# A sparse 3x3 convolution on one core: every image stored in two halves of 32 rows, and the last pair's load issued whole with the others

## The chip, the cores and the metric

The kernel runs on one core of a Trainium2 chip. Its time is the device time of one execution in microseconds. Three executions of the kernel before took 127.68, 127.80 and 127.81 us, median 127.8 us.

## The reference

Sixteen images of 64 channels and 64 x 64 pixels are convolved with 128 filters of 3 x 3, padded by one. Nine weights in ten are zero, but the kernel multiplies by all of them. All inputs and outputs are 32-bit floats in HBM.

```python
batch, c_in, h, w, c_out, k = 16, 64, 64, 64, 128, 3
x_pad = np.pad(x, ((0, 0), (0, 0), (1, 1), (1, 1)))
for b, co, ci, kh, kw in all_indices:
    output[b, co] += weight[co, ci, kh, kw] * x_pad[b, ci, kh:kh+h, kw:kw+w]
```

## The kernel before, in words

**Pairs and blocks.** The images are worked off in eight pairs, p = 0 to 7. The 64 channels of the pair's two images fill the 128 partitions, and each image uses half of TensorE's rows. Each image is cut into four blocks of 16 rows. A block called "T" (`twos`, L151) computes even and odd output rows apart: GpSimd (POOL) adds neighbouring rows of x (L154, tile `s`), TensorE multiplies (L135), ScalarE (ACT) copies the shared product to SBUF (L161, tile `pc`), and VectorE (DVE) adds it to the rest and writes the output tile `o` (L168). The first block of pair 0 goes a direct way (`direct`, L144).

**Loads.** Pair 0's upper half is loaded as floats by SyncE's queue (SP, L62) and cast by engines. Everything else of x is loaded by GpSimd's queue with a cast to 16 bits on the way: pair 0's lower half (L63), pairs 1 to 6 whole (L67), all issued at the start; then pair 7, whose three DMAs (L177 to L181) stand in the program at the head of pair 2, and so in GpSimd's stream behind the row additions of pair 1. They load the upper half of the rows for all 128 partitions, and the lower half once for partitions 0 to 7 and once for partitions 8 to 127. Every pair has its own x tile, so no load waits for a buffer.

**Stores.** An image's output is a tile of 128 partitions x 64 x 64 floats, 2 MB, 16 KB in each partition. There are seven such buffers (pool `o`, L47); the first holds the head of x at the start, and image j uses buffer (j + 1) modulo 7, so image j can be written only when the stores of image j - 7 have landed. Images of pairs 0 to 6 are stored whole behind the pair's last block (L193 to L195). Only the two images of pair 7 go in halves of 32 rows, each behind its second and fourth block (L189 to L192). All stores go through SyncE's queue, which also waits there for VectorE.

**Order.** The scheduling is manual: every engine works in the order of the program, and only the waits on semaphores tie them. The transfers of both queues run on the same 16 DMA engines. On the SP queue a store uses one of eight completion semaphores in turn.

Of the kernel before, what the change touches and what calls it, by code (L numbers as in the profile page):

```python
# [27 lines left out]
def kernel(  # L28
# [6 lines left out]
    nc = tc.nc  # L35

    B, C_IN, H, W = x.shape
    C_OUT, _, KH, KW = weight.shape
    assert (B, C_IN, H, W) == (16, 64, 64, 64) and (C_OUT, KH, KW) == (128, 3, 3)
    NP = B // 2  # L40
# [14 lines left out]
    def pair(p):  # L55
        return x[2 * p : 2 * p + 2].rearrange("n i h w -> (n i) h w")

    xs = [x_pool.tile([128, H, W], BF16, name=f"x{p}") for p in range(NP)]
# [4 lines left out]
    nc.gpsimd.dma_start(out=xs[0][:, HEAD:H, :], in_=pair(0)[:, HEAD:H, :])  # L63
    ident = const_pool.tile([128, 128], BF16, name="ident")
    make_identity(nc, ident)
    for p in range(1, NP - 1):
        nc.gpsimd.dma_start(out=xs[p], in_=pair(p))  # L67


# [74 lines left out]
    def direct(p, o, r0, rows):  # L144
        ps = product(
            [(xs[p], G1, r0, 1), (xs[p], G0, r0 - 1, 1), (xs[p], G2, r0 + 1, 1)], rows
        )
        nc.scalar.copy(out=o[0][:, r0 : r0 + rows, :], in_=ps[0])  # L148
        nc.vector.tensor_copy(out=o[1][:, r0 : r0 + rows, :], in_=ps[1])  # L149

    def twos(p, o, r0):  # L151
        t0 = r0 // 2
        s = s_pool.tile([128, 8, W], BF16, name="s")
        nc.gpsimd.tensor_tensor(  # L154
            out=s, in0=xs[p][:, r0 : r0 + 16 : 2, :], in1=xs[p][:, r0 + 1 : r0 + 16 : 2, :], op=ADD
        )
        shared = product([(s, G1, 0, 1)], 8)
        pc = []
        for n in range(2):
            c = p_pool.tile([128, 8, W], FP32, name="pc")  # L160
            nc.scalar.copy(out=c, in_=shared[n])  # L161
            pc.append(c)
        even = [(xs[p], G21, r0 + 1, 2), (xs[p], G0, r0 - 1, 2)]
        odd = [(xs[p], G01, r0, 2), (xs[p], G2, r0 + 2, 2)]
        for first, terms in ((r0, even), (r0 + 1, odd)):
            ps = product(terms, 8)
            for n in range(2):
                nc.vector.tensor_tensor(  # L168
                    out=o[n][:, first : r0 + 16 : 2, :], in0=ps[n], in1=pc[n], op=ADD
                )  # L170

    for p in range(NP):
        o = [o_pool.tile([C_OUT, H, W], FP32, name="o") for _ in range(2)]
        last = p == NP - 1
        if p == 2:
            x_last, half = pair(NP - 1), H // 2
            nc.gpsimd.dma_start(out=xs[NP - 1][:, 0:half, :], in_=x_last[:, 0:half, :])  # L177
            for a, b in ((0, 8), (8, 128)):
                nc.gpsimd.dma_start(  # L179
                    out=xs[NP - 1][a:b, half:H, :], in_=x_last[a:b, half:H, :]  # L180
                )  # L181
        for blk in range(4):
            r0 = 16 * blk
            if BLOCKS[p][blk] == "T":
                twos(p, o, r0)
            else:
                for r, rows in ((r0, 8), (r0 + 8, 8)):
                    direct(p, o, r, rows)
            if last and blk % 2 == 1:  # L189
                for n in range(2):  # L190
                    rows = slice(r0 - 16, r0 + 16)
                    nc.sync.dma_start(out=out[2 * p + n][:, rows, :], in_=o[n][:, rows, :])  # L192
        if not last:  # L193
            for n in range(2):
                nc.sync.dma_start(out=out[2 * p + n], in_=o[n])  # L195


# [28 lines left out]
```

## Time and profile before

| | |
|---|---|
| median of three executions | 127.8 us |
| the profiled execution: time | 127.8 us |
| the profiled execution: span, first to last instruction | 126.0 us |
| granted TensorE clock, mean | 0.958 |
| TensorE matmul busy | 110.5 us (88%) |
| VectorE, ScalarE, GpSimd busy | 82.3, 38.9, 41.8 us |
| HBM read, written | 17.07 MB, 33.55 MB |
| a whole-image store, from issue to landing (median of 14) | 17.6 us |
| a half-image store (median of 4) | 10.1 us |

Times in the views are microseconds from the span's start. In the page's strip of 40 slices one slice is 3.15 us; its line DMA gives the mean busy share of the 16 DMA engines in tenths, and GB/s what they moved, where a load that is cast counts with its 16-bit size only, half of what it reads. PE is TensorE, SPq and POOLq are the instruction queues of SyncE and GpSimd that issue DMAs. A DMA is cut into packets of one partition's row each; beside the views the trace keeps a record of every packet (queue, start, duration, size) and of every completion, and numbers said to be of the packet records are read there.

### The profile page before, as it was taken

The page shows a single profiled execution, that of the slowest core. Times are in us where ns is not written, and L with a number is a line of the kernel's source. Part 1 is how long each engine was busy: PE and PEld are TensorE (multiplying, and loading weights), DVE is VectorE, ACT ScalarE, POOL GpSimd, SP SyncE. Part 2 cuts the span into 40 slices and gives each one's busy share as a digit, 9 for nine tenths or more (in the row PEclk, how much of TensorE's full clock was granted, in tenths as well). Part 3 has the DMA queues.
Part 4 walks back from the last instruction along what each step waited for, and adds up shares of the span by engine and source line. Part 5 has one row for each costly group of instructions (what it writes and reads, how often), then busy time and mean ns, then how long its engine had stood idle before and what let it go on. Part 6 is the DMA issues. An engine that isn't in the chain of part 4 may idle for free.

```text
span 126.0 us, 2489 instructions
## 1 busy us (share of the span) xinstructions
PE 110.5 (88%) x1002; PEld 56.0 (44%) x1002; DVE 82.3 (65%) x135; ACT 38.9 (31%) x71; POOL 41.8 (33%) x47
## 2 busy tenths in 40 slices
PE   6679999999999999999999999999999999990000
PEld 6434445544555455545554555445544554440000
DVE  0352277777777777877787778777877787773000
ACT  4541532333333333333333333333333333330000
POOL 6846333383333333333333333333333330000000
PEclk9999999999999999999999999999999999998555
DMA  4999999999999999999999999999999999999980
GB/s 140 343 229 211 216 213 216 221 164 296 325 335 302 325 296 371 344 376 351 367 412 426 421 432 432 437 429 416 421 437 437 411 400 437 437 390 413 432 343 21
DMA packets 4220, 42.93 MB, mean 341 GB/s; under 512 B 496, under 2 KB 496, under 8 KB 1008
## 3 DMA queue, kind: packets, MB, share of 16 engines
q1 hardware_dynamic: 2880, 34.90, 65.9%
q0 software_dynamic: 1328, 7.87, 30.9%
q8 instruction: 8, 0.13, 0.4%
q14 instruction: 4, 0.03, 0.1%
HBM read 17.07 MB, written 33.55 MB: 402 GB/s over the span
## 4 chain that ended last, share of the span: by engine, by line
PE 83%; DMA 4%; DVE 1%; issue 1%; DVEq 0%; SPq 0%
PE ps L135 83%; DMA o<-in_x_dram 4%; DVE o L168 1%; DVEq L221 0%; DVE x L87 0%; SPq L60 0%; DVEq L168 0%
## 5 line engine op out<-in xcount | busy, mean ns | idle before, releaser
L135 PE MATMUL ps<-x,wT 64*128 64x504 bf16 (+3 forms) x780 | 91.5, 382 | 1.6 <-DVE x L87 1.6
L168 DVE TENSOR_TENSOR o<-ps,pc 128x512 f32<-128x512 f32 x124 | 77.8, 685 | 22.1 <-PE ps L135 19.8
L135 PEld LDWEIGHTS <-wT 64*128 64x128 bf16 x966 | 52.5, 96 | 55.2 <-issue 5.0
L154 POOL TENSOR_TENSOR s<-x 128x512 bf16<-128x512 bf16 x31 | 35.6, 1151 | 59.5 <-PE ps L135 46.7
L161 ACT COPY pc<-ps 128x512 f32<-128x512 f32 x62 | 33.3, 589 | 64.0 <-issue 61.8
L135 PE MATMUL ps<-s,wT 64*128 64x512 bf16 (+1 forms) x186 | 25.5, 377 | 0.0
L149 DVE COPY o<-ps 128x512 f32<-128x512 f32 x2 | 1.4, 692 | 4.9 <-PE ps L135 4.9
L74 PE MATMUL ps<-idle_rhs 128*128 128x128 bf16 x27 | 3.1, 310 | 1.0 <-DVE idle_rhs L71 1.0
L74 PEld LDWEIGHTS <-idle_rhs 128*128 128x128 bf16 x27 | 2.8, 144 | 1.0 <-DVE idle_rhs L71 1.0
L67 POOL DMA_DIRECT2D x<-in_x_dram x6 | 3.2, 560 | 0.0
L91 DVE CAST w_bf<-w_sb 128x192 bf16<-128x192 f32 (+1 forms) x4 | 1.1, 361 | 2.7 <-DMA w_sb<-in_weight_dram 2.7
L148 ACT COPY o<-ps 128x512 f32<-128x512 f32 x2 | 1.2, 585 | 5.3 <-PE ps L135 5.3
L87 ACT CAST x<-o 128x576 bf16<-128x576 f32 (+1 forms) x2 | 1.5, 802 | 0.6 <-DMA o<-in_x_dram 0.6
L87 DVE CAST x<-o 128x576 bf16<-128x576 f32 x1 | 0.5, 459 | 1.7 <-DMA o<-in_x_dram 1.7
L91 ACT ACT_TABLE_LOAD x1 | 1.3, 1283 | 0.7 <-PEq L210 0.7
L97 PE MATMUL ps<-ident,w_bf 128*128 128x128 bf16 x9 | 1.2, 308 | 0.1
L91 ACT CAST w_bf<-w_sb 128x64 bf16<-128x64 f32 (+1 forms) x2 | 0.7, 418 | 1.6 <-DMA w_sb<-in_weight_dram 1.6
L179 POOL DMA_DIRECT2D x<-in_x_dram x2 | 1.1, 530 | 0.0
L97 PEld LDWEIGHTS <-w_bf 128*128 128x128 bf16 x9 | 0.8, 127 | 0.6 <-DVE w_bf L91 0.6
L101 DVE TENSOR_TENSOR wT<-ps,wT 128x384 bf16<-128x384 f32 x2 | 1.0, 546 | 0.0
L63 POOL DMA_DIRECT2D x<-in_x_dram x1 | 0.7, 710 | 0.8 <-POOLq L210 0.8
L71 DVE MEMSET idle_rhs<- 128x64 uint32 x1 | 0.1, 112 | 0.8 <-PEq L210 0.8
(10 smaller groups left out, 3.0 us busy)
## 6 DMA issues: line engine op xcount, KB each, us to landing
out_dram<-o SPq DMA_DIRECT2D x14, 2048.0 KB, 17.6
x<-in_x_dram POOLq DMA_DIRECT2D x6, 1024.0 KB, 23.9
out_dram<-o SPq DMA_DIRECT2D x4, 1024.0 KB, 10.1
o<-in_x_dram SPq DMA_DIRECT2D x1, 1024.0 KB, 5.3
x<-in_x_dram POOLq DMA_DIRECT2D x2, 512.0 KB, 20.2
x<-in_x_dram POOLq DMA_DIRECT2D x1, 480.0 KB, 40.3
w_sb<-in_weight_dram SPq DMA_DIRECT2D x1, 288.0 KB, 2.9
x<-in_x_dram POOLq DMA_DIRECT2D x1, 32.0 KB, 33.4
```

What stands on the lines that cost most here:

```text
L67: nc.gpsimd.dma_start(out=xs[p], in_=pair(p))
L74: nc.tensor.matmul(idle_ps, idle_rhs, idle_rhs, start=True, stop=True)
L87: copy(out=xs[0][:, a:b, :], in_=x_head[:, a:b, :])
L91: copy(out=w_bf4[:, g, a:b, :], in_=w_v[:, k : k + b - a, :])
L97: nc.tensor.matmul(wps[:, j, :], src, ident, start=True, stop=True)
L135: nc.tensor.matmul(ps[n][:, lo:hi, c_lo:c_hi], tap(g, kw, n), src[q, a:b:step, c_lo + kw - 1 : c_hi + kw - 1], start=(i == 0), stop=(i == ...
L148: nc.scalar.copy(out=o[0][:, r0 : r0 + rows, :], in_=ps[0])
L149: nc.vector.tensor_copy(out=o[1][:, r0 : r0 + rows, :], in_=ps[1])
L154: nc.gpsimd.tensor_tensor(out=s, in0=xs[p][:, r0 : r0 + 16 : 2, :], in1=xs[p][:, r0 + 1 : r0 + 16 : 2, :], op=ADD)
L161: nc.scalar.copy(out=c, in_=shared[n])
L168: nc.vector.tensor_tensor(out=o[n][:, first : r0 + 16 : 2, :], in0=ps[n], in1=pc[n], op=ADD)
L179: nc.gpsimd.dma_start(out=xs[NP - 1][a:b, half:H, :], in_=x_last[a:b, half:H, :])
```

## The change

All seven later pairs are now loaded at the start by the loop at L66, each with one DMA; the three DMAs at the head of pair 2 are gone. Every image is stored in two halves, where only pair 7's were: behind a pair's second block two DMAs send rows 0 to 31 of both images, and behind its fourth block two more send rows 32 to 63. There are 32 stores of 1 MB in place of 14 of 2 MB and 4 of 1 MB.

```diff
-    for p in range(1, NP - 1):
+    for p in range(1, NP):
         nc.gpsimd.dma_start(out=xs[p], in_=pair(p))
...
         o = [o_pool.tile([C_OUT, H, W], FP32, name="o") for _ in range(2)]
-        last = p == NP - 1
-        if p == 2:
-            x_last, half = pair(NP - 1), H // 2
-            nc.gpsimd.dma_start(out=xs[NP - 1][:, 0:half, :], in_=x_last[:, 0:half, :])
-            for a, b in ((0, 8), (8, 128)):
-                nc.gpsimd.dma_start(
-                    out=xs[NP - 1][a:b, half:H, :], in_=x_last[a:b, half:H, :]
-                )
...
-            if last and blk % 2 == 1:
+            if blk % 2 == 1:
                 for n in range(2):
                     rows = slice(r0 - 16, r0 + 16)
                     nc.sync.dma_start(out=out[2 * p + n][:, rows, :], in_=o[n][:, rows, :])
-        if not last:
-            for n in range(2):
-                nc.sync.dma_start(out=out[2 * p + n], in_=o[n])
```

## The prediction

> **What bounds the kernel now.** I read the page's strip first. PE is full from 7 to 113 us, but the DMA line is full from 3 to 122 us, and after the last matmul the engines move bytes for some ten microseconds more.
>
> ```profile
> PE   6679999999999999999999999999999999990000
> DMA  4999999999999999999999999999999999999980
> GB/s 140 343 229 211 216 213 216 221 164 296 325 335 302 325 296 371 344 376 351 367 412 426 421 432 432 437 429 416 421 437 437 411 400 437 437 390 413 432 343 21
> q1 hardware_dynamic: 2880, 34.90, 65.9%
> q0 software_dynamic: 1328, 7.87, 30.9%
> ```
>
> The two queues' packets take 96.8% of the 16 engines' time in the span; 216 GB/s of cast loads are 432 GB/s read. So the loads and stores, one after the other, make the time, if nothing starves them. I looked for that in SyncE's waits and then in the windows.
>
> ```profile
> SPq L195 <- DVE o L168: 93.7, 14, 22.7
> SPq L192 <- DVE o L168: 10.5, 4, 5.3
> SPq L221 <- DMA out_dram<-o: 8.8, 4, 2.4
> ```
>
> The store queue waits for VectorE, never for a buffer, and VectorE waits for no store. After the last issue the program only waits for stores (L221).
>
> ```profile
> 24.00:26.00 2.00, 2.00 (x22) 1.05 (x20) 1.40 (x3) 1.07 (x2) 1.61 (x2) 1.00 1.01 209
> 26.00:28.00 2.00, 2.00 (x22) 0.98 (x20) 2.00 (x4) 0.55 (x2) 1.55 (x4) 1.00 1.08 143
> 28.00:30.00 2.00, 2.00 (x22) 0.96 (x18) 1.27 (x4) 0.52 (x2) 0.69 (x1) 1.00 0.95 250
> 68.00:100.00 32.00, 32.00 (x302) 16.02 (x300) 25.02 (x41) 10.74 (x20) 11.53 (x10) 1.00 1.00 427
> 100.00:102.00 2.00, 2.00 (x24) 1.05 (x20) 1.77 (x3) 0.88 (x2) 0.78 (x1) 1.00 0.93 393
> 114.00:121.00 7.00, 0.00 (x0) 0.00 (x0) 0.58 (x1) 0.00 (x0) 0.00 (x0) 0.60 1.01 421
> ```
>
> The last two columns are the DMA share and GB/s. Whole-image stores run at 427 GB/s (68 to 100), half-image stores at 421 (114 to 121). There are two weak places: a dip to 143 GB/s at 26 to 28 with the engines marked busy, and a share of 0.93 at 100 to 102, just before pair 6's stores are issued (101.2). By the packet records this is one engine idle for 2.5 us and a few others for 0.3 us.
>
> ```profile
> 24.39 1.15 POOL L154 TENSOR_TENSOR s<-x 128x512 bf16<-128x512 bf16 x1 [2.02 <-PE ps L135]
> 24.42 0.88 SPq L195 DMA_DIRECT2D out_dram<-o  x2
> 25.48 0.57 POOL L177 DMA_DIRECT2D x<-in_x_dram  x1
> 26.04 1.05 POOL L179 DMA_DIRECT2D x<-in_x_dram  x2
> ```
>
> The timeline at the dip: SyncE has just issued the first stores, GpSimd issues pair 7's loads. In the packet records the 69 load packets that start between 25.3 and 29.5 take 843 ns in the mean instead of 625, up to 1515, until the first store packet starts at 28.84. That is 69 x 218 / 16 = 0.94 us lost on every engine.
>
> **The change part by part.** The sum is made on the profiled execution (127.8 us, span 126.0, so 1.8 us lie outside); it is also the median.
>
> *Stores in halves.* A store packet of 16 KB takes 614.8 ns in the mean (66 to 106 us), one of 8 KB 310.2 (116 us to the end). Each engine carries 8 rows of each of the 14 images, 112 packets, which become 224: 112 x (2 x 310.2 - 614.8) = 0.63 us; 14 more completion packets of 9 ns make 0.13. Engines that only store confirm it: one image every 4.862 us, one half every 2.453, so 14 x 0.044 = 0.61. From the windows, 29.4 MB at 421 instead of 427 GB/s is 69.8 - 68.8 = 1.0 us. I take 0.6, bounds 0 to 1.0. It lies on the path, because no engine has idle time for it. A rule of the Trainium skill speaks against halves: "DMA: Bandwidth & Descriptors", Anatomy of one DMA, gives a transfer of GpSimd's path a fixed 2.0 us besides its bytes. If each of 14 added stores paid that, the time would be 28 us longer; the half-stores at 421 GB/s above show it overlapped while more is queued.
>
> *Earlier stores.* Pair 0's first halves can go at 18.5 us (VectorE's last addition of the second block) in place of 24.4. More is queued, but a full pipe moves no more for it. The idle 0.3 us at 102 goes, on engines that do not end last: worth nothing. At the end pair 7's second halves are issued at 114.0 and 114.6 as now, and their turn comes about 2 x 2.45 before the last landing at 124.9, so at 120: 5 us of cover, nothing gained.
>
> *The order of loads.* Pair 7's load was queued behind pairs 3 to 6 already; on its queue it stays there. GpSimd issues it at 5.72 for some 0.56 us, inside 2.39 us of idle before its additions at 8.11: nothing. If issuing blocked on an eighth outstanding load it would delay TensorE from 13.75 on. The 1.6 us gone from GpSimd's stream at 25.5 end in waits for free s buffers: nothing either.
>
> *How loads and stores share.* While both run, packets alternate: at 30 to 54 us some 27 of stores to 26 of loads in 2 us. With 8 KB against 16 KB read, stores get a third of the time instead of half until the loads end. Loads come earlier (each x tile lands two pairs ahead already), stores later. By the packet records a pair's load alone takes 4.88 us, and pair 3's ends at 23.3. If the first store packet comes at 22 (some 3.5 us behind its issue; it was 4.4), 1.3 + 4 x 4.88 = 20.8 us of loads are left, so both run until 22 + 1.5 x 20.8 = 53, and 10.4 / 2.45 = 4.2 half-stores are done by then. The third lands at 44, the seventh at 60, the sixteenth at 82, one each 2.45 us. Image 9 needs image 2's buffer (the seventh) at 63.7 (VectorE begins pair 1 at 25.5 and a pair every 12.75): 3.4 us of slack, the tightest case. If that cover went, VectorE and then TensorE would stop, and 5 us at the end hide it. A store also needs its completion semaphore, used eight stores earlier: the twelfth may wait 1.5 us in SyncE with seven queued behind it on the engines, which costs nothing.
>
> *The load itself.* Three DMAs become one. A 16 KB read takes 624 ns beside stores and an 8 KB read 322, so 8 x (2 x 322 - 624) = 0.16 us less per engine. The rows of 0 to 7 that some engines carry on top go: 0 or 0.32 us, by engine. Sum -0.2, bounds 0 to -0.5. The engine spared eight rows (8 x 0.31 = 2.5 us, just its idle time at 100) gets them back and stands among the others. "DMA: Bandwidth & Descriptors", How many engines (k), says that 120 partitions of such a load can go to engines 0 to 14 alone, which would name it the sixteenth; no view here numbers engines.
>
> *The dip.* Who makes it, the trace does not say. For the first stores: it ends on each engine as its first store packet starts. Against GpSimd's issuing: the six issues of L67 end at 5.72 and the load packets of 5.3 to 7.5 take 332 ns against 324, nearly nothing. So I let it move with the first stores to about 19 us: cost 0, bounds -0.9 to +0.3 (stores and loads start up differently).
>
> Sum: 0.6 - 0.2 + 0 = +0.4, so 128.2 us; the bounds of the first terms give 127.9 to 128.6.
>
> **The rivals.**
> 1. *The dip belongs to the load that is moved.* GpSimd starts issuing at 25.48 and the first long packets start at 25.41 to 26.1. Then 0.9 us go: 128.2 - 0.9 = 127.3, faster. Against it stand the rows at 5.3 to 7.5.
> 2. *The spared engine becomes the last one.* The sixteen completions of the last store lie between 122.2 and 124.9, the second latest at 124.1: single engines are late, among them by instruction fetches of 16 KB (eight in the span, about 0.9 us each). If the engine that gets eight rows back is one of these, it ends behind them: price 0 to 2.5, taken as 0.8, so 129.0. It decides once that engine's other work is over 2 us above the others'; in the trace, less its spare, it stands in the middle.
> 3. *Nothing to be seen.* Half rows cost nothing when stores always queue deep, and the rows saved balance the rest: 127.8.
>
> **How the numbers follow.** A measurement of this kernel tells about 0.2% (0.26 us) from no change. The forecast gets 0.55, rival 1 0.25, rival 2 0.12, rival 3 0.08. Faster: rival 1 nearly whole and a little of the forecast, 0.27. Within 0.2%: rival 3, about a fifth of the forecast, a trace of rival 1, 0.20. Slower: the rest, 0.53. The range reaches to rival 1 and to most of rival 2: 127.2 to 128.9; the forecast's own is 127.9 to 128.6.
>
> **What would show it.** In the changed profile: the strip's DMA line full as now; a dip near 19 to 22 us and none at 26 (rival 1: none at all); 421 GB/s in place of 427 in the pure store stretch, which should begin near 53 instead of 65; no share of 0.93 at 100; PE ending at 112 to 113; no wait of VectorE for a store; SyncE waiting for stores once or twice near 50. A PE line with holes, a load issue of over 1 us on GpSimd, or an engine whose completions trail by over 3 us would make the prediction wrong.

## The result and the profile after

The changed kernel takes 128.43 us (median of 4, 128.38 to 128.51) against 127.81 us before on the same chip: +0.62 us, ratio 1.0045 with the 95% interval 1.0024 to 1.0066. It is slower, as forecast (+0.4), by a little more than the sum. Ratios leave out the executions over 1.5% above the fastest of the same kernel, which run in a slower state of the chip, and so need not be the quotient of the medians. The profiled execution took 128.47 us with a span of 126.5.

The strip and the queues of the page of the changed kernel:

```profile
PE   6669999999999999999999999999999999900000
DMA  4999999999999999999999999999999999999960
GB/s 144 333 224 212 218 194 262 282 295 272 290 274 285 287 280 290 280 355 419 432 427 417 422 435 419 422 430 419 419 438 417 419 430 427 419 425 427 422 293 10
q1 hardware_dynamic: 4896, 34.90, 66.5%
q0 software_dynamic: 1152, 7.86, 30.3%
```

The DMA line is as full as before, from 3 to 122 us. TensorE ends in slice 35, the transfers in slice 39; they still set the end. The bytes are the same, the store queue has 4896 packets in place of 2880, and the GB/s line shows the second stretch, stores alone, beginning at slice 19 (57 us) where it began at slice 21 (63 us). Slices are counted from one.

Windows of the changed kernel (last two columns: DMA share, GB/s):

```profile
16.00:18.00 2.00, 2.00 (x22) 1.02 (x18) 1.45 (x3) 0.25 (x1) 0.48 (x1) 1.00 1.01 188
18.00:20.00 2.00, 2.00 (x22) 1.07 (x20) 1.27 (x3) 1.07 (x2) 1.15 (x1) 1.00 1.02 213
68.00:100.00 32.00, 32.00 (x304) 17.07 (x302) 25.16 (x41) 10.75 (x20) 11.53 (x10) 1.00 1.01 423
100.00:102.00 2.00, 2.00 (x22) 1.02 (x18) 2.00 (x4) 0.37 (x1) 0.00 (x0) 1.00 1.05 442
114.00:121.00 7.00, 0.00 (x0) 0.00 (x0) 0.00 (x0) 0.00 (x0) 0.00 (x0) 0.54 1.01 428
```

The dip is there at 16 to 19 us, where the first store packet starts (19.03), and no longer at 26 to 28; it is shallower, 188 GB/s against 143. Stores alone run at 423 GB/s against 427 while the compute engines work; at the very end, 114 to 121, they reach 428. The share of 0.93 at 100 us is gone.

What SyncE waited for, in the changed kernel (us in total, times, longest):

```profile
SPq L184 <- DVE o L168: 68.6, 27, 13.6
SPq L184 <- DMA out_dram<-o: 26.9, 12, 6.9
```

The store queue now waits for earlier stores, twelve times, up to 6.9 us, where it never did; with stores under way the engines do not notice, and the DMA line stays full.

VectorE, too, waited once for a store, where it had not before. The line of its waits, and its timeline there:

```profile
DVE o L168 <- DMA out_dram<-o: 0.4, 1, 0.4
62.39 1.89 DVE L168 TENSOR_TENSOR o<-ps,pc 128x512 f32<-128x512 f32 x3 [0.42 <-DMA out_dram<-o]
```

It is image 9, which needs image 2's buffer: the second half of image 2 landed at 62.20 us, and VectorE had been ready since 61.97. TensorE did not stop for it.

**The ledger.** The durations of all packets, summed and divided by 16 engines, are the load of one engine:

| | store queue | load queue | both | last landing | time of this execution |
|---|---|---|---|---|---|
| before | 83.08 | 38.94 | 122.02 | 124.87 | 127.8 |
| after | 84.13 | 38.30 | 122.43 | 125.27 | 128.47 |
| difference | +1.05 | -0.64 | +0.41 | +0.40 | +0.67 |

The sum of both queues and the last landing moved alike, by 0.41 and 0.40 us. That they agree to 0.01 us is closer than the method goes: the sum is a mean over 16 engines, the last landing that of the one engine which ends last (the median of the sixteen last completions moved from 122.85 to 123.10, by 0.25). How far the two agree in the other kernels stands at the end of the experiments. The remaining 0.27 us lie behind the last landing (the span's rest grew from 1.16 to 1.28) and outside the span (from 1.77 to 1.92); of these I have no cause, and executions of one kernel differ by as much.

### The profile page after: what moved, and what is told of

It is laid out like the page before. It is cut to its first block, busy times and chain, and to the rows that moved or that the text cites. A ratio compares the mean times of both kernels' runs of the same rounds, so it can differ in the third digit from the quotient of the medians.

```text
span 126.5 us, 2523 instructions
## 1 busy us (share of the span) xinstructions
PE 107.5 (85%) x1002; PEld 58.3 (46%) x1002; DVE 82.3 (65%) x135; ACT 39.0 (31%) x71; POOL 40.8 (32%) x45
## 3 DMA queue, kind: packets, MB, share of 16 engines
q1 hardware_dynamic: 4896, 34.90, 66.5%
## 4 chain that ended last, share of the span: by engine, by line
PE 81%; DMA 4%; DVE 1%; issue 1%; DVEq 0%; SPq 0%
PE ps L135 81%; DMA o<-in_x_dram 4%; DVE o L168 1%; DVEq L210 0%; DVE x L87 0%; SPq L60 0%; DVEq L168 0%
## 5 line engine op out<-in xcount | busy, mean ns | idle before, releaser
L168 DVE TENSOR_TENSOR o<-ps,pc 128x512 f32<-128x512 f32 x124 | 77.8, 685 | 22.1 <-PE ps L135 19.4
L135 PE MATMUL ps<-x,wT 64*128 64x504 bf16 (+3 forms) x780 | 88.8, 373 | 1.8 <-DVE x L87 1.8
L135 PEld LDWEIGHTS <-wT 64*128 64x128 bf16 x966 | 54.8, 94 | 50.1 <-issue 1.8
L135 PE MATMUL ps<-s,wT 64*128 64x512 bf16 (+1 forms) x186 | 25.7, 377 | 0.0
L67 POOL DMA_DIRECT2D x<-in_x_dram x7 | 3.7, 560 | 0.0
L63 POOL DMA_DIRECT2D x<-in_x_dram x1 | 0.7, 698 | 0.8 <-POOLq L199 0.8
L110 ACT CAST wT<-ps 128x384 bf16<-128x384 f32 x1 | 0.5, 479 | 0.3 <-PE ps L97 0.3
```

Of the source, the lines that this page charges most:

```text
L135: nc.tensor.matmul(ps[n][:, lo:hi, c_lo:c_hi], tap(g, kw, n), src[q, a:b:step, c_lo + kw - 1 : c_hi + kw - 1], start=(i == 0), stop=(i == ...
L168: nc.vector.tensor_tensor(out=o[n][:, first : r0 + 16 : 2, :], in0=ps[n], in1=pc[n], op=ADD)
```

## The experiments

Theory: the time follows the packet time on the DMA engines; halves cost there, the load's new form saves a little, the dip goes with the first stores. Rivals: the dip belongs to the load that is moved; the engine that was spared eight rows is the one that ends last.

**Halves only.** Pair 7's loads stay in pair 2 as before.

```diff
-            if last and blk % 2 == 1:
+            if blk % 2 == 1:
...
-        if not last:
-            for n in range(2):
-                nc.sync.dma_start(out=out[2 * p + n], in_=o[n])
```

> Only the halves, pair 7's load as before (three DMAs from within pair 2). Theory (8 KB packets cost more, the dip comes with the first stores): 112 x 5.6 ns + 14 completions = 0.6 to 0.75 us over before, so 128.4 to 128.6; the dip is near 16 to 20 us, and when GpSimd issues pair 7's loads near 25 us, with stores already running, load packets stay near 624 ns. Rival (the load's issue makes the dip): long load packets at 25 to 29 us, and the time at 128.4 or more. Rival (the spared engine is the reason for the slower time): 127.8, as before.

Measured: 128.68 us, ratio 1.0072 (1.0050 to 1.0094), so 0.9 us over before. The median lies further above before than that of the whole change (1.0045), though the two intervals overlap. Windows of this kernel:

```profile
20.00:22.00 2.00, 2.00 (x22) 1.02 (x20) 1.92 (x4) 0.67 (x2) 0.58 (x1) 1.00 1.02 156
22.00:24.00 2.00, 2.00 (x22) 1.03 (x20) 1.35 (x3) 0.40 (x1) 0.57 (x1) 1.00 0.99 279
24.00:26.00 2.00, 2.00 (x22) 1.08 (x20) 1.40 (x3) 1.07 (x2) 1.41 (x2) 1.00 1.00 287
26.00:28.00 2.00, 2.00 (x22) 0.97 (x19) 2.00 (x4) 0.35 (x1) 1.55 (x4) 1.00 1.14 303
```

GpSimd issues pair 7's three loads at 25.7 to 27.3 here (the 1.55 us of POOL with four instructions in the last row), and the rate does not fall: load packets that start at 24 to 28 take 624 ns. The dip stands at 20 to 22, ahead of the first store packet at 22.1. The first rival falls. The store queue's packets sum to 84.24 us an engine. The spared engine runs some 2 us ahead of the median from 58 us to the end here and never idles, and the time is no better for it; another engine ends last, 1.4 us behind the next. So the slower time does not come from giving that engine its eight rows back: the second rival falls too, and the next kernel, which gives them back, is no slower than before.

**The load only.** Pair 7 whole at the start, stores as before.

```diff
-    for p in range(1, NP - 1):
+    for p in range(1, NP):
...
-        if p == 2:
...
```

> Only the load changed: pair 7 whole at the start with the others, stores as before. Theory: load packets are still long at 26 to 29 us, though GpSimd issues no load there; time 127.8 less 0 to 0.3, since three DMAs become one. Rival (the load's issue makes the dip): packets of 625 ns throughout and 126.9. Rival (the spared engine becomes the last): 128.3 or more.

Measured: 127.65 us, ratio 0.9990 (0.9967 to 1.0013). Windows of this kernel:

```profile
22.00:24.00 2.00, 2.00 (x24) 1.06 (x21) 1.40 (x4) 0.56 (x2) 0.74 (x1) 1.00 1.05 205
24.00:26.00 2.00, 2.00 (x22) 1.08 (x20) 1.27 (x4) 1.07 (x2) 1.15 (x1) 1.00 1.05 197
26.00:28.00 2.00, 2.00 (x22) 1.07 (x20) 2.00 (x4) 0.11 (x1) 0.01 (x1) 1.00 1.00 299
```

Without any load issued there, load packets of some 750 ns in the mean (up to 1360) still precede the first store packet at 25.7: a dip of 0.70 us an engine. In the GB/s it is flat, since it lies across two rows. It follows the first stores, which were issued earlier here (21.6 us instead of 24.4) because the first block was multiplied in 4.0 us instead of 6.9. In packet time the load queue gets 0.42 us shorter, 0.24 of it the dip; in the median of the times the gain is 0.1 us and within the interval of none.

**The changed kernel with the split load, issued at the start.**

```diff
-    for p in range(1, NP):
+    for p in range(1, NP - 1):
         nc.gpsimd.dma_start(out=xs[p], in_=pair(p))
+    x_last, half = pair(NP - 1), H // 2
+    nc.gpsimd.dma_start(out=xs[NP - 1][:, 0:half, :], in_=x_last[:, 0:half, :])
+    for a, b in ((0, 8), (8, 128)):
+        nc.gpsimd.dma_start(out=xs[NP - 1][a:b, half:H, :], in_=x_last[a:b, half:H, :])
```

> The changed kernel, with pair 7 loaded at the start by the three DMAs of before (the lower half as 8 and 120 partitions). It gives the one engine its eight rows less again. Theory: that engine is not the last to end, so the time stays at 128.4 to 128.6 and one engine's completions run some 2.5 us ahead of the others at 70 us. Rival (the spared engine is the one that ends last): 127.8.

Measured: 128.94 us, ratio 1.0094 (1.0075 to 1.0112). Nobody expected that, and the kernel tests something else than was meant. GpSimd's timeline in it:

```profile
5.65 0.58 POOL L69 DMA_DIRECT2D x<-in_x_dram  x1
9.23 0.52 POOL L71 DMA_DIRECT2D x<-in_x_dram  x1 [3.00 <-DMA x<-in_x_dram]
14.11 0.53 POOL L71 DMA_DIRECT2D x<-in_x_dram  x1 [4.35 <-DMA x<-in_x_dram]
14.65 4.46 POOL L158 TENSOR_TENSOR s<-x 128x512 bf16<-128x512 bf16 x4
```

GpSimd takes its completion semaphores from a set of eight, too: in the records the ten loads complete on eight semaphores, and two of these are used twice. The ninth and tenth load wait until the first and second have landed (8.96 and 13.82 us), and the row additions queue behind them until 14.65 instead of 8.4. TensorE ends at 115.6, the last two stores are issued at 117.6, and the engines run dry:

```profile
116.00:118.00 2.00, 0.77 (x8) 0.22 (x4) 2.00 (x4) 0.00 (x0) 0.00 (x0) 1.00 0.82 336
```

The DMA share is 0.82 at 116 to 118, and thirteen of the sixteen last completions lie within 0.1 us at 123.8. So the cover of some 5 us at the end is real, and this delay of 3 to 6 us uses it up. The changed kernel issues eight loads and stays just inside the set.

**Quarters.** The cost enlarged: stores of 16 rows in the changed kernel.

```diff
-            if blk % 2 == 1:
+            if True:
...
-                    rows = slice(r0 - 16, r0 + 16)
+                    rows = slice(r0, r0 + 16)
```

> The changed kernel with stores of 16 rows, 64 of 512 KB, packets of 4 KB: the suspected cost enlarged. A packet of 16 KB took 611 ns, one of 8 KB 309, so a packet costs some 7 ns besides its bytes: 128 x 4 x 158 - 128 x 2 x 309 ns is 1.8 us, and 32 completions of 9 ns 0.3, so 2.1 us over the changed kernel: 130.5. If the cost of a store lies in its packets less than in the first stores' dip or the load, it stays under 129.

Measured: 130.38 us, ratio 1.0209 (1.0189 to 1.0228); 1.95 us over the changed kernel, 2.1 forecast. Splitting costs again. That the size came out is partly luck: a packet of 4 KB takes 160.8 ns alone and 169 beside loads, not 158, so the store queue's sum rose by 3.08 us and that of both queues by 2.79, while the last landing moved by only 2.00. The durations count too much here:

```profile
68.00:100.00 32.00, 32.00 (x302) 17.00 (x300) 25.00 (x41) 10.74 (x20) 11.52 (x10) 1.00 1.03 417
```

They add up to 1.03 of the engines' time in this stretch, so packets overlap; the rate fell from 423 to 417 GB/s. VectorE waited twice for a store (3.8 us in all, the longer one 3.2) and TensorE's strip has one gap near 53 us, but it ended at 111.8 us with the DMA share still full.

**Where the halves cost more than forecast.** Two kernels with the new load, halves in pairs 0 to 2 or in pairs 3 to 6 (pair 7 in halves in both). The edit of the first against the load-only kernel:

```diff
-            if last and blk % 2 == 1:
+            if (last or p < 3) and blk % 2 == 1:
...
-        if not last:
+        if not (last or p < 3):
```

The second has the conditions `p > 2` and `p <= 2` in these places.

> Load as in the changed kernel, halves only for pairs 0 to 2 and 7, whole stores for pairs 3 to 6. Theory (beside loads a packet of 16 KB became 18 ns dearer by halving, alone 6.6 ns): six images, of which some 21 packets an engine run beside loads: 21 x 18 + 27 x 6.6 ns + 0.06 = 0.62 us more store packet time than the load-only kernel, less 0.1 to 0.4 of a smaller dip; 127.9 to 128.2. Rival (the same price for every half, wherever it runs): 6/14 of 0.9 = 0.4 us of packet time.

> Load as in the changed kernel, halves only for pairs 3 to 7, whole stores for pairs 0 to 2. Theory: eight images that run alone: 64 x 6.6 ns + 0.08 of completions = 0.5 us more store packet time than the load-only kernel, dip as there (0.7): 128.1. Rival (the same price for every half): 8/14 of 0.9 = 0.5 to 0.6; it is told apart by the kernel with halves in pairs 0 to 2.

Measured: 128.15 us (1.0041, 1.0027 to 1.0054) and 128.05 us (1.0025, 1.0011 to 1.0038). Against the load-only kernel's 82.96 the store queue's packets sum to 83.72 and 83.52 us an engine: 0.76 for six images and 0.56 for eight. Without the first 10 us, in which this queue carries only loads that no edit touches, it is 0.63 (0.105 an image) and 0.53 (0.066), as the theory said (0.62 and 0.5), where one price for every half asked for 0.4 and 0.5 to 0.6. So a half is dearer where it runs beside loads, by about 1.6 times. The times do not show this: with the smaller dip of the first (0.43 us against 0.74) both queues sum to 122.01 and 122.04 us, and the two intervals overlap.

**Whole stores throughout.** The load-only kernel with pair 7 stored whole as well: the store of the whole image behind the block loop is all that is left.

> Load as in the changed kernel, and every image stored whole, pair 7's too. Theory: two images fewer in halves save 2 x 0.044 = 0.1 us of packet time if pair 7's stores are issued before pair 6's end (near 114); issued at 111 to 115, they just miss or make it, so 127.5 to 128.4, and a share of the DMA line under 0.9 near 114 where they miss it. Rival (halves cost nothing by themselves, something else in the change does): no change of the store packet time, 127.65.

Measured: 127.91 us, ratio 1.0016 (0.9998 to 1.0033). The strip of this kernel:

```profile
DMA  4999999999999999999999999999999999968993
```

In slices 36 and 37 (110 to 117 us) the engines are short of work, and all sixteen last completions lie between 124.36 and 124.74, where those of the load-only kernel lie between 121.6 and 124.2. Pair 7's whole stores come too late. The store queue's sum is 82.96 us in both, though 0.1 less was forecast; kernels with the same stores differ by as much (83.08 before, 82.96 load only, 83.14 with the other order of loads below), so this kernel does not show what two images cost. In the median of the times halves for pair 7 are worth 0.26 us, with intervals that overlap; for the other pairs no such cover is needed, since their stores are issued while others are still queued.

**The spared engine.** The kernel before with the two part loads in the other order, and the load-only kernel with one store of pair 7 in two parts.

```diff
-            for a, b in ((0, 8), (8, 128)):
+            for a, b in ((0, 120), (120, 128)):
```

> The kernel before with the order of the two lower-half loads exchanged: partitions 0 to 119 first, then 120 to 127. In the kernel before one engine was spared eight rows and ran 2.5 us ahead until it idled at 100 us, while another one trailed at the end by 0.7 us (and by 1.3 to 1.9 us where nothing was spared or the halves were added). Theory: the order decides which engine is spared. If it is now the trailing one, the last landing moves forward by 0.7 to 1.5 us, to 127.0 to 126.4; if it is a third engine, the time stays at 127.8 and the spared one again idles near 100 us. Rival (the spare has no part in the end): 127.8 in either case with the same trailing engine.

```diff
-                    nc.sync.dma_start(out=out[2 * p + n][:, rows, :], in_=o[n][:, rows, :])
+                    parts = ((0, 120), (120, 128)) if (blk, n) == (1, 0) else ((0, 128),)
+                    for a, b in parts:
+                        nc.sync.dma_start(
+                            out=out[2 * p + n][a:b, rows, :], in_=o[n][a:b, rows, :]
+                        )
```

(The condition stands under that for pair 7, and holds for the first half of image 14, rows 0 to 31; the expectation names the second. A further kernel has `((0, 8), (8, 128))` in its place.)

> The load-only kernel, with one half-store of pair 7 (image 14, rows 32 to 63) as two DMAs, partitions 0 to 119 and 120 to 127. That spares one of the 16 engines eight packets, 2.45 us, at a place where no idle time follows. One engine trailed the others by 1.6 us at the end of the load-only kernel. Theory: if the spared engine is that one, the last landing comes 1.2 us earlier, 126.4; if it is another, it ends 2.5 us ahead, eight others carry one packet more (0.31 us), and the time is 127.6 to 128.0. Rival (no engine is last by itself, the stores end together): 127.65.

> As the kernel with the split store, but partitions 0 to 7 first and then 8 to 127, so that the engines carry other partitions in this one store. If the trailing goes with the engine, the result is that of the other order; if the spared engine changes with the order, one of the two kernels may reach 126.4. Else 127.6 to 128.0.

Measured: the other order of loads, 127.84 us, ratio 1.0009 (0.9996 to 1.0021): again one engine runs 3.3 us ahead until pair 6's stores start, and another trails the median by 1.7 us at the end. The split stores: 130.30 us (1.0179, 1.0133 to 1.0224) and 129.31 us (1.0073, 1.0032 to 1.0114; its executions spread from 127.84 to 130.50), both missed. In the one an engine trails the median of the last store by 3.8 us, in the other by 2.8. Packets of 8 KB take 335 and 337 ns in the mean instead of 309 to 312; those that start at 111 to 119 us, around the split store, take up to 1278 and 1291 ns, those behind them 309 to 311 again. Sparing an engine this way never reached the one that trails, and the store on fewer than 128 partitions had slower packets around it in both kernels. Why, no run here shows.

**A small first store.** The load-only kernel, with pair 0's first 16 rows stored by themselves.

```diff
+            if p == 0 and blk == 0:
+                for n in range(2):
+                    nc.sync.dma_start(out=out[n][:, 0:16, :], in_=o[n][:, 0:16, :])
...
+            lo = 16 if p == 0 else 0
             for n in range(2):
-                nc.sync.dma_start(out=out[2 * p + n], in_=o[n])
+                nc.sync.dma_start(out=out[2 * p + n][:, lo:H, :], in_=o[n][:, lo:H, :])
```

> The load-only kernel, but pair 0's first 16 rows are stored by themselves behind the first block (packets of 4 KB), its other 48 rows together (12 KB). Theory (the dip before the first store packet grows with the size of the packets that start: 0.7 to 1.1 us an engine for 16 KB, 0.3 to 0.7 for 8 KB, 0.2 for 4 KB): the dip falls from 0.7 to about 0.2, 16 packets more an engine cost 0.1 to 0.3, so 127.2 to 127.5. Rival (the dip is the same for whatever stores come first, its size being chance): 127.7 to 127.9, dip 0.5 to 1.0.

Measured: 127.41 us, ratio 0.9947 (0.9922 to 0.9973), faster than before and after. Windows of this kernel:

```profile
14.00:16.00 2.00, 2.00 (x22) 0.98 (x18) 1.20 (x2) 0.50 (x2) 1.10 (x1) 1.00 1.04 209
16.00:18.00 2.00, 2.00 (x22) 0.99 (x19) 1.31 (x3) 1.07 (x2) 1.15 (x1) 1.00 0.99 203
18.00:20.00 2.00, 2.00 (x22) 1.03 (x20) 1.97 (x4) 0.04 (x1) 0.00 (x0) 1.00 0.99 260
```

The first store packet starts at 16.9, and the dip ahead of it is 0.26 us an engine, as the theory said. What made the time shorter is not shown all the same: against the load-only kernel the dip is 0.44 us less, but the store queue's sum is 0.44 more (83.40 against 82.96), both queues together 0.25 more and the last landing 0.26 later. (The profiled execution of the load-only kernel was the fastest of its twelve, 127.25 us.)

**The same, meant to be later.** The two small stores stand behind the fourth block in the program; the edit is against the kernel with the small first store.

```diff
-            if p == 0 and blk == 0:
+            if p == 0 and blk == 3:
```

> As the kernel with the small first store, but those 16 rows of pair 0 are sent only behind its fourth block, right ahead of the other 48 rows. Size and moment of the first store are told apart: if the size of the first packets makes the dip, it stays near 0.2 to 0.4 and the time at 127.3 to 127.6; if the moment does (first stores early, while fewer loads are under way), the dip is 0.7 to 1.1 as with 16 KB packets, and the time 127.6 to 128.0.

Measured: 127.55 us, ratio 0.9974 (0.9957 to 0.9992), dip 0.23 us. But the first store packet starts at 17.1, as early as in the kernel before it: SyncE has no other store ahead of them and issued them at 13.6 us (13.4 in the kernel before it), as soon as the 16 rows were written. So this is a repetition and not the separation that was meant; its ratio overlaps with that of the load-only kernel (0.9967 to 1.0013). Whether size or moment makes the dip small stays open; one pair of rows speaks for size: at nearly the same moment, halves at 25.0 us had a dip of 0.31 (the split load at the start), whole stores at 25.7 one of 0.70 (load only).

**The ledger over all kernels.** Sum of both queues' packets an engine, and last landing, each against before (us):

| kernel | packets | last landing |
|---|---|---|
| changed kernel | +0.41 | +0.40 |
| halves only | +0.84 | +0.75 |
| load only | -0.54 | -0.62 |
| split load at the start | +0.70 | +0.82 |
| quarters | +3.20 | +2.40 |
| halves in pairs 0 to 2 and 7 | -0.01 | +0.28 |
| halves in pairs 3 to 7 | +0.02 | +0.18 |
| whole stores throughout | -0.19 | -0.13 |
| other order of loads | 0.00 | -0.10 |
| split store, 120 first; 8 first | +0.52; +0.93 | +2.18; +1.68 |
| small first store; its repetition | -0.28; -0.24 | -0.36; -0.34 |

Eight of the thirteen agree to some 0.1 us. With halves in a part of the pairs the landing moved by 0.2 to 0.3 us that the sum does not have, in the quarters by 0.8 us less, in the split stores by 0.75 and 1.7 us more. So the sum tells the direction and the rough size, and what the engine that ends last does on top stays open.

## Why the prediction was right, point by point

**The bound** was right: the DMA engines stayed full and the end moved with their packet time (0.41 us an engine, last landing 0.40), within the limits of the table above. TensorE shows it from the other side: it ended at 109.4 us instead of 112.0, because its first 36 matmuls took 4.0 us instead of 6.9, and the kernel got slower all the same. Before, and in the changed kernel:

```profile
7.03 6.89 PE L135 MATMUL ps<-x,wT 64*128 64x512 bf16 x36 [1.63 <-DVE x L87]
7.29 3.99 PE L135 MATMUL ps<-x,wT 64*128 64x512 bf16 x36 [1.82 <-DVE x L87]
```

In the load-only kernel TensorE was early, too, in the halves-only kernel not (6.7 us), and in others it took 5.5 to 5.7; no run here shows why.

**The halves** were sized too low: 0.6 forecast, 0.94 measured. The store queue's sum rose by 1.05 us, of which 0.79 lie in the packets of the stores and 0.15 in their completions; 0.11 lie in the loads that this queue makes in the first 10 us and that the change does not touch. The step that failed is "112 x (2 x 310.2 - 614.8)" and "I take 0.6". The completions, 0.13 by the prediction's own line, were left out of the 0.6; and the prices are those of packets that run alone, taken for all 112. Alone they came out as said (2 x 310.8 - 615.0 = 6.6 ns). Beside loads a packet of 8 KB takes 320.3 ns and one of 16 KB 622.6, so a split costs 18 ns, and the 667 half packets there make 21 such pairs an engine: 21 x 18 = 0.38, the other 91 x 6.6 = 0.60, 14 completions of 10.5 ns 0.15, in sum 1.13. Two things take off some 0.2 of it: fewer stores ran beside loads (21 packets of 16 KB or their halves an engine instead of 38, 17 x 7.3 ns = 0.12), and pair 7's own halves took 310.2 ns instead of 313.0 (0.09). For whole packets beside loads the trace of before had the price (623.8 ns at 30 to 54 us); for halves there it had none, since its halves ran behind the loads. The rule of the Trainium skill that was weighed there ("DMA: Bandwidth & Descriptors", Anatomy of one DMA, a fixed 2.0 us for a transfer of GpSimd's path) would, as an estimate, have made it 28 us for the 14 added stores; these go through SyncE's queue, and queued this deep they cost 0.94.

**The load's form** was right: -0.2 forecast, -0.24 left of the load queue's -0.64 when the dip's -0.40 is taken out (load only: -0.18 of -0.42).

**The dip** did move with the first stores, as the forecast had it and rival 1 did not. But its price was put at 0, and it came out at -0.40: 0.94 us before, 0.55 after. It lay within the bounds of -0.9 to +0.3. The wrong terms cancelled: +0.34 for the halves and +0.11 in the first loads against -0.40 for the dip; that the sum of 0.4 came so near the ledger's 0.41 is luck. Nor do the forecast's own 127.9 to 128.6 follow from its terms: 0 to 1.0 and -0.5 to 0 give 127.3 to 128.8. The measured 128.43 lies in both.

**The sharing** was right as far as the loads go: by the packet records they end at 54 to 56 us (53 forecast). The slack of 3.4 us for image 9, called the tightest case, was gone: image 2's second half landed at 62.2 us instead of 60, and VectorE, started earlier by TensorE, wanted the buffer at 62.0 instead of 63.7, so it waited 0.42 us. It cost nothing, as the prediction said of this case, since TensorE ended ahead of the engines by more. Too small was the wait on completion semaphores: 26.9 us in twelve waits in place of once or twice 1.5. It cost nothing either, for the reason given.

**Rival 1** (0.25) was refuted by the halves-only kernel: pair 7's loads were issued at 25.7 us and no dip came there. **Rival 2** (0.12) was refuted by the halves-only kernel and by the load-only one, which gives the eight rows back and takes 127.65 us where the rival asked for 128.3 or more. **Rival 3** would have asked for an unchanged store sum of 83.08.

**The signs set out**: the full DMA line, no dip at 26 us, no share of 0.93 at 100 and no hole in TensorE's strip held. The dip came at 16 to 19 us instead of 19 to 22, the stretch of stores alone began at 57 us instead of 53 and ran at 423 GB/s instead of 421, TensorE ended at 109.4 us instead of 112 to 113, SyncE waited twelve times, and VectorE once.

## What to carry to other kernels

Where the DMA engines are full from the first load to the last store, sum the packets' durations by queue before and after: that sum moved by 0.41 us and the last landing by 0.40, while earlier stores and an earlier end of TensorE bought nothing. Take it for the direction and the rough size: in five of thirteen kernels here the landing went some 0.2 us or more apart from it. Price a split transfer with packets that run in the company it will have: beside loads the halving cost nearly three times as much per packet as alone. Cut only where the cut gives cover, at the last pair, and perhaps at the very first store: with a small first store the median was the lowest here (127.41 us, 127.55 in the repetition, 127.65 without it), but the packet sums do not explain it.

## What the runs showed of the hardware that was not expected

- Before the first store packet starts, load packets under way on the same engines stretch from 625 ns up to 1606. The loss was 0.70 to 1.08 us an engine ahead of packets of 16 KB (seven kernels), 0.31 to 0.67 ahead of 8 KB (four), 0.22 to 0.26 ahead of 4 KB (three).
- One engine trails. In the changed kernel the latest completion of each half comes every 2.60 us between 85 and 110 us, against 2.45 on the others, and at the common pace once TensorE has ended; it lands 1.9 us behind the next at the end. It does so with no load in flight. The instruction fetches do not make it: only two fall in that stretch (0.94 and 0.31 us), and the pace is even. Which engine it is and what it shares, no run here shows.
- The ninth load outstanding on GpSimd's queue blocked GpSimd for 3.0 us and the tenth for 4.35, each until an earlier load had landed.
